# Hybrid SSD and pooling decoder step: the first transfers and splits in smaller pieces, warm-up matmuls between the first real ones

## The chip, the cores and the metric

The kernel runs on one core of a Trainium2 chip. The metric is the device time of one execution in microseconds (us), the median of several runs. The engines are named as in the profile: PE (TensorE: matmuls, with PEld for its weight loads), DVE (VectorE), ACT (ScalarE), POOL (GpSimd) and SP (SyncE, which issues nearly all DMAs here). A granted clock of 1.00 is PE's full speed.

## What is computed

One inference step of a one-layer decoder with two branches: a Mamba-2 style state-space branch (SSD) and a causal pooling branch, joined by sigmoid gates. There are 336 token rows (16 meta, 256 prompt, 64 sample). What matters here is the beginning: the tokens, weighted by `norm_w`, are multiplied by the input projection.

```
h = concat(meta_tokens, x_prompt), x_sample          # 336 rows x 2048
xn = h * rsqrt(mean(h*h) + 1e-6) * norm_w
proj = xn @ w_in                                     # 2048 -> 13344 columns
z_ssd, xbc, dt_raw, z_pool, u, gates = split(proj)
xbc -> causal conv (4 taps), silu -> xs, B, C
dt = softplus(dt_raw + dt_bias); SSD scan over xs, B, C, dt; group norm, w_proj_ssd
pooling means over 2, 4, 8, 16 rows of u; mix, scale, silu(z_pool), w_proj_pool
out = rms_norm(h + (gate_ssd * branch_ssd + gate_pool * branch_pool) @ w_out)
```

## The kernel before

All weights are cut into units of 128 output columns. A unit has 2048 input rows, that is 16 tiles k of 128, and is stored in two halves of 8 tiles (128 x 1024 f32, 512 KB). The order of the units is fixed in `UNITS`; the first are B 0 to 3, C 0 to 3, then xs.

Products are made nearly exact by splitting. A weight half `raw` is rounded by ACT to fp32r (`hi`, line 145), and DVE subtracts to get the rest (`lo`, line 151). The tokens, in 16 tiles of 128 x 336 (`xg`, four tiles in each of four groups; shown as x in the profile), are scaled by `norm_w` and split in the same way into `wh` and `wl`, shown as xh and xl (lines 238 to 249): tile 4q of a group on DVE, the other three on ACT, and all four rests on DVE. Each product of a unit with a tile is three matmuls: hi with xh, hi with xl, lo with xh.

The row scale 1/rms is applied only to the results, so the matmuls can begin before the sum of squares is known. That sum (`sq`, lines 284 to 292) is formed later and read by PE in `ps_sumx` (line 163), in the middle of unit 2.

Units 0 and 1 are run together (lines 251 to 279). For each group q of four tiles PE does 24 matmuls into `acc2`, then four f32 matmuls with the small weight `wdt` for the step sizes, into `psd` (shown as ps_dt). From unit 2 on the loop at the end of the function runs one unit after the other and prepares weights ahead (`prep_hi`, `prep_lo`, `load_to`).

The order on each engine is that of the program (`manual_schedule`), and each engine works through its own list in order, waiting on semaphores where data is missing. SP keeps at most eight of these DMAs under way: from the ninth on, each waits in the compiled program for the DMA eight places before it. The pools `raw`, `hi` and `lo` have four buffers each, so the load of unit 2's first half waits until the first `raw` has been read for the last time.

Before the data is there, PE runs `NWARM` matmuls of a matrix of ones (lines 224 and 225, shown as ps_warm). A copy of that result into `pbs` (line 259) on DVE keeps them in use; `pbs` is overwritten later (line 865).

Of the kernel before, what the change touches and what calls it, by code (L numbers as in the profile page):

```python
# [67 lines left out]
def hybrid_step(tc, ctx, io):  # L68
    nc = tc.nc
    V, S, PE, GP, SY = nc.vector, nc.scalar, nc.tensor, nc.gpsimd, nc.sync  # L70

# [69 lines left out]

    def prep_hi(i, h):
        r = raws[i, h]
        hi = wp.tile([128, HW], F32R, tag="hi", name=f"hi{i}_{h}")
        S.activation(hi, r, AF.Copy)  # L145
        whl[i, h] = hi

    def prep_lo(i, h):
        r, hi = raws.pop((i, h)), whl[i, h]
# [1 line left out]
        V.tensor_tensor(out=lo, in0=r, in1=hi.bitcast(F32), op=ALU.subtract)  # L151
# [60 lines left out]
    load_to(3)
    SY.dma_start(out=xg[2], in_=io["xT"][:, 8:12, :])
    load_to(4)
    SY.dma_start(out=xg[3], in_=io["xT"][:, 12:16, :])
# [5 lines left out]
    load_to(7)  # L221
    V.memset(ones, 1.0)
    warm = ps.tile([128, 512], F32, tag="st", name="ps_warm")
    for j in range(NWARM):
        PE.matmul(warm[:, 0:128], lhsT=ones, rhs=ones, start=(j == 0), stop=(j == NWARM - 1))
# [12 lines left out]
    def split_hi(q):
        for c in range(4):
            k = 4 * q + c  # L240
            if c:
                S.activation(wh[q][:, c, :], xg[q][:, c, :], AF.Copy, scale=pc("norm_w", k))
            else:
                V.tensor_scalar(out=wh[q][:, c, :], in0=xg[q][:, c, :], scalar1=pc("norm_w", k), scalar2=None, op0=ALU.mult)

    def split_lo(q):
        for c in range(4):
            V.scalar_tensor_tensor(out=wl[q][:, c, :], in0=xg[q][:, c, :], scalar=pc("norm_w", 4 * q + c),
                                   in1=wh[q][:, c, :].bitcast(F32), op0=ALU.mult, op1=ALU.subtract)

    for q in range(4):
        h = q // 2
        if q == 0:
# [5 lines left out]
            V.tensor_copy(out=pbs, in_=warm[:, 0:16])
# [2 lines left out]
        else:
            split_hi(q)
            if q < 3:
                prep_hi(q - 1, 1)
            split_lo(q)
            if q < 3:
                prep_lo(q - 1, 1)
        for part in range(3):
            for u in range(2):  # L270
                w = whl[u, h]
                for c in range(4):
                    k = 4 * q + c
                    cc = slice(128 * (k % 8), 128 * (k % 8) + 128)
                    PE.matmul(acc2[u][:, :T], lhsT=w[part // 2][:, cc], rhs=(wl if part == 1 else wh)[q][:, c, :],  # L275
                              start=(k == 0 and part == 0), stop=(k == 15 and part == 2))
        for c in range(4):
            PE.matmul(psd[32 * c:32 * c + 32, :T], lhsT=wdt[:, 4 * q + c, :], rhs=xg[q][:, c, :], start=(q == 0),
                      stop=(q == 3), skip_group_check=True, tile_position=(0, 32 * c))
# [794 lines left out]
```

## Time and profile before

| what | value |
| --- | --- |
| median of 3 runs | 1217.36 us (1216.51 to 1217.37) |
| profiled execution: time / span | 1220.42 / 1218.6 us |
| mean granted PE clock | 0.991 |
| PE busy | 1197.0 us (98%) |
| DVE busy | 739.4 us (61%) |
| ACT busy | 540.1 us (44%) |
| first warm-up matmul, first real matmul | 1.06 us, 7.20 us |
| DMA | 202.49 MB, mean 166 GB/s |

The page gives the busy time of each engine, and then the chain of work that ended last, followed back from the last instruction. The timeline lists instructions in order of time with the idle time ahead of them and what ended it; an f32 matmul is two records in it, an fp32r matmul one. Busy times of PE include the modelled tail of a pipelined matmul, about 0.3 us, so the start of the next one tells more than a duration.

### The profile page before, as it was taken

The page shows a single profiled execution, that of the slowest core. Times are in us where ns is not written, and L with a number is a line of the kernel's source. Part 1 is how long each engine was busy: PE and PEld are TensorE (multiplying, and loading weights), DVE is VectorE, ACT ScalarE, POOL GpSimd, SP SyncE. Part 2 cuts the span into 40 slices and gives each one's busy share as a digit, 9 for nine tenths or more (in the row PEclk, how much of TensorE's full clock was granted, in tenths as well). Part 3 has the DMA queues.
Part 4 walks back from the last instruction along what each step waited for, and adds up shares of the span by engine and source line. Part 5 has one row for each costly group of instructions (what it writes and reads, how often), then busy time and mean ns, then how long its engine had stood idle before and what let it go on. Part 6 is the DMA issues. An engine that isn't in the chain of part 4 may idle for free.

```text
span 1218.6 us, 19976 instructions
## 1 busy us (share of the span) xinstructions
PE 1197.0 (98%) x8124; PEld 1169.4 (96%) x8124; DVE 739.4 (61%) x1141; ACT 540.1 (44%) x735; POOL 105.2 (9%) x107
## 2 busy tenths in 40 slices
PE   8999999999999999999999999999999999999995
PEld 7999999888899999999999999999999999999995
DVE  7786998987885643443457475665354355554443
ACT  6455746474754533333233443434443333334441
POOL 0001151625161000000000000000000000000000
PEclk9999999998999999999999999999999999999997
DMA  7555556574655444444456455454444444455432
GB/s 279 181 159 172 182 169 240 161 247 150 247 174 179 140 155 151 145 154 152 144 172 167 153 155 162 149 166 156 149 146 156 150 146 155 151 189 197 150 111 86
DMA packets 83075, 202.49 MB, mean 166 GB/s; under 512 B 26615, under 2 KB 31639, under 8 KB 82967
## 3 DMA queue, kind: packets, MB, share of 16 engines
q1 hardware_dynamic: 82823, 200.19, 49.2%
q8 instruction: 63, 1.03, 0.3%
q0 software_dynamic: 160, 1.03, 0.2%
q14 instruction: 29, 0.24, 0.1%
HBM read 186.34 MB, written 15.32 MB: 165 GB/s over the span
## 4 chain that ended last, share of the span: by engine, by line
PE 85%; DVE 6%; DMA 4%; issue 2%; ACT 1%; POOL 1%; SPq 0%; DVEq 0%; POOLq 0%
PE acc L231 27%; PE acc L230 27%; PE acc L232 27%; DMA bc<-acT 3%; DVE lo L151 2%; PE acc L275 1%; DVE cacc L337 1%; DMA raw<-wall 1%; DVE M L547 1%; DVE hin L646 1%; DVE hn L969 0%; DMA ossms<-hin 0%; POOL hin L638 0%; PE ps_y L593 0%; PE ps_hn L644 0%
## 5 line engine op out<-in xcount | busy, mean ns | idle before, releaser
L145 ACT ACTIVATE hi<-raw 128x1024 fp32r<-128x1024 f32 x312 | 330.2, 1059 | 542.6 <-PE acc L231 387.5
L151 DVE TENSOR_TENSOR lo<-raw,hi 128x1024 fp32r<-128x1024 f32 x312 | 387.0, 1241 | 258.9 <-ACT hi L145 258.9
L230 PE MATMUL acc<-xh,hi 128*128 128x320 f32 (+4 forms) x1632 | 511.2, 313 | 0.0
L231 PE MATMUL acc<-xl,hi 128*128 128x320 f32 (+4 forms) x1632 | 508.5, 312 | 0.0
L232 PE MATMUL acc<-xh,lo 128*128 128x320 f32 (+4 forms) x1632 | 507.2, 311 | 0.0
L230 PEld LDWEIGHTS acc<-xh,hi 128*128 128x128 f32 x1632 | 307.4, 188 | 2.5 <-issue 0.8
L231 PEld LDWEIGHTS acc<-xl,hi 128*128 128x128 f32 x1632 | 307.3, 188 | 1.1
L232 PEld LDWEIGHTS acc<-xh,lo 128*128 128x128 f32 x1632 | 307.6, 188 | 0.0
L230 PE MATMUL acc<-mh,hi 128*128 128x320 f32 x256 | 79.2, 309 | 0.0
L231 PE MATMUL acc<-ml,hi 128*128 128x320 f32 x256 | 79.1, 309 | 0.0
L232 PE MATMUL acc<-mh,lo 128*128 128x320 f32 x256 | 79.1, 309 | 0.0
L231 PE MATMUL acc<-pl,hi 128*128 128x320 f32 x256 | 79.0, 308 | 0.0
L231 PE MATMUL acc<-yl,hi 128*128 128x320 f32 x256 | 78.9, 308 | 0.0
L232 PE MATMUL acc<-yh,lo 128*128 128x320 f32 x256 | 78.9, 308 | 0.0
L232 PE MATMUL acc<-ph,lo 128*128 128x320 f32 x256 | 78.9, 308 | 0.0
L230 PE MATMUL acc<-yh,hi 128*128 128x320 f32 x256 | 78.9, 308 | 0.0
L230 PE MATMUL acc<-ph,hi 128*128 128x320 f32 x256 | 78.9, 308 | 0.0
L638 POOL TENSOR_TENSOR hin<-hin,E 128x512 f32<-128x512 f32 x32 | 49.7, 1581 | 42.5 <-ACT E L556 42.5
L337 DVE SCALAR_TENSOR_TENSOR cacc<-rawf,par,cacc 128x360 f32<-128x360 f32 (+1 forms) x72 | 48.2, 669 | 1.8
L231 PEld LDWEIGHTS acc<-ml,hi 128*128 128x128 f32 x256 | 48.1, 188 | 0.0
L230 PEld LDWEIGHTS acc<-mh,hi 128*128 128x128 f32 x256 | 48.1, 188 | 0.0
L231 PEld LDWEIGHTS acc<-pl,hi 128*128 128x128 f32 x256 | 48.1, 188 | 0.0
(222 smaller groups left out, 1215.3 us busy)
## 6 DMA issues: line engine op xcount, KB each, us to landing
raw<-wall SPq DMA_DIRECT2D x312, 512.0 KB, 3.3
hin<-ssmT SPq DMA_DIRECT2D x16, 512.0 KB, 6.4
ossms<-hin SPq DMA_DIRECT2D x16, 512.0 KB, 5.6
bc<-acT SPq DMA_DIRECT2D x8, 672.0 KB, 7.2
hn<-xT SPq DMA_DIRECT2D x4, 640.0 KB, 7.7
x<-xT SPq DMA_DIRECT2D x3, 672.0 KB, 9.3
opool<-u SPq DMA_DIRECT2D x16, 100.0 KB, 3.0
oconv<-rawf SPq DMA_DIRECT2D x24, 45.5 KB, 4.1
```

The lines of the kernel that those rows point to most:

```text
L145: S.activation(hi, r, AF.Copy)
L151: V.tensor_tensor(out=lo, in0=r, in1=hi.bitcast(F32), op=ALU.subtract)
L230: PE.matmul(acc[:, :n], lhsT=hi[:, c], rhs=bh, start=first, stop=False)
L231: PE.matmul(acc[:, :n], lhsT=hi[:, c], rhs=bl, start=False, stop=False)
L232: PE.matmul(acc[:, :n], lhsT=lo[:, c], rhs=bh, start=False, stop=last)
L275: PE.matmul(acc2[u][:, :T], lhsT=w[part // 2][:, cc], rhs=(wl if part == 1 else wh)[q][:, c, :], start=(k == 0 and part == 0), stop=(k == ...
L337: V.scalar_tensor_tensor(out=a[:, a0:], in0=r[:, a0 + k:k + ACCW], scalar=pc("conv_w", 4 * c + k), in1=a[:, a0:], op0=ALU.mult, op1=ALU.add)
L547: V.tensor_scalar(out=m[:n, e, o:o + hi - lo], in0=b[:n, hh % 4, lo:hi], scalar1=act_[:n, i, h0 + hh:h0 + hh + 1], scalar2=0.0, op0=ALU.su ...
L638: GP.tensor_tensor(out=hv, in0=hv, in1=E, op=ALU.mult)
L646: later(1, lambda: V.tensor_tensor(out=h, in0=h, in1=p, op=ALU.add))
```

## The change

It touches only what stands ahead of unit 2:

- `par` is loaded in two pieces: the 16 columns of `norm_w` first, the other 264 after all x tiles.
- The first halves of units 0 and 1 and then their second halves are loaded and split in pieces of 512 columns (four k tiles), alternating between the units. The x tiles come singly (0 and 1) or in pairs.
- Splits are issued per quarter and per x tile, in the order in which the matmuls use them.
- `NWARM` goes from 16 to 11. Twelve more warm-up matmuls stand each behind one real matmul of x tiles 0 and 1, six more behind those of tiles 2 and 3. The copy into `pbs` stays behind the last of them.
- In group 0 the order is by pairs of tiles, then unit, then part; in the later groups by part, pair and unit. The step-size matmuls of group 0 move behind group 1.

```diff
-NACC, NTR, NWARM = 3, 3, 16
+NACC, NTR, NWARM = 3, 3, 11
...
-    SY.dma_start(out=par, in_=io["par"])
-    load_to(1)
-    SY.dma_start(out=xg[0][:, 0:2, :], in_=io["xT"][:, 0:2, :])
-    SY.dma_start(out=xg[0][:, 2:4, :], in_=io["xT"][:, 2:4, :])
-    load_to(2)
-    SY.dma_start(out=xg[1], in_=io["xT"][:, 4:8, :])
+    def load_x(k, n):
+        SY.dma_start(out=xg[k // 4][:, k % 4:k % 4 + n, :], in_=io["xT"][:, k:k + n, :])
+
+    def load_part(i, h, a):
+        if not a:
+            raws[i, h] = wp.tile([128, HW], F32, tag="raw", name=f"raw{i}_{h}")
+        SY.dma_start(out=raws[i, h][:, 512 * a:512 * a + 512], in_=io["wall"][i, h, :, 512 * a:512 * a + 512])
+
+    SY.dma_start(out=par[:, 0:16], in_=io["par"][:, 0:16])
+    load_part(0, 0, 0)
+    load_x(0, 1)
+    load_x(1, 1)
+    load_part(1, 0, 0)
+    load_x(2, 2)
+    load_part(0, 0, 1)
+    load_part(1, 0, 1)
+    load_x(4, 2)
+    load_x(6, 2)
     SY.dma_start(out=wdt, in_=io["wdt"])
...
+    for j in range(2):
+        load_part(0, 1, j)
+        load_part(1, 1, j)
+        load_x(8 + 4 * j, 2)
+        load_x(10 + 4 * j, 2)
+    SY.dma_start(out=par[:, 16:NPAR], in_=io["par"][:, 16:NPAR])
+    nload[0] = 4
...
-    for j in range(NWARM):
-        PE.matmul(warm[:, 0:128], lhsT=ones, rhs=ones, start=(j == 0), stop=(j == NWARM - 1))
+    def turn_over(n):
+        for j in range(n):
+            PE.matmul(warm[:, 0:128], lhsT=ones, rhs=ones, start=True, stop=True)
+    turn_over(NWARM)
...
     for q in range(4):
-        h = q // 2
         if q == 0:
-            prep_hi(0, 0)
-            split_hi(0)
-            prep_hi(1, 0)
-            split_lo(0)
-            prep_lo(0, 0)
+            w_hi(0, 0)
+            x_hi(0)
+            x_lo(0)
+            x_hi(1)
+            w_lo(0, 0)
+            x_lo(1)
+            w_hi(1, 0)
+            w_lo(1, 0)
+            x_hi(2)
+            x_lo(2)
+            x_hi(3)
+            x_lo(3)
+            for k, u in ((0, 0), (0, 1), (2, 0), (2, 1)):
+                for part in range(3):
+                    for d in range(2):
+                        mm(u, k + d, part)
+                        if k == 0:
+                            turn_over(1)
+            turn_over(6)
             V.tensor_copy(out=pbs, in_=warm[:, 0:16])
-            prep_lo(1, 0)
+        else:
+            for u in range(2):
+                w_hi(u, q)
+                w_lo(u, q)
+            for k in range(4 * q, 4 * q + 4):
+                x_hi(k)
+                x_lo(k)
+            for part in range(3):
+                for k in range(4 * q, 4 * q + 4, 2):
+                    for u in range(2):
+                        mm(u, k, part)
+                        mm(u, k + 1, part)
+        if q == 1:
             V.tensor_tensor(out=wdt, in0=wdt, in1=par[:, o:o + 16].unsqueeze(2).to_broadcast([128, KT, NH]), op=ALU.mult)
...
+        for e in ((), (0, 1), (2,), (3,))[q]:
+            for c in range(4):
+                PE.matmul(psd[32 * c:32 * c + 32, :T], lhsT=wdt[:, 4 * e + c, :], rhs=xg[e][:, c, :], start=(e == 0),
+                          stop=(e == 3), skip_group_check=True, tile_position=(0, 32 * c))
```

`x_hi`, `x_lo`, `w_hi` and `w_lo` are the old splits for one x tile or one quarter, and `mm` is one matmul.

What stands where, on the two engines that matter. Names read as tile, unit or group, half: raw0_0 is unit 0, first half; xh1 is group 1. On PE at its beginning, before:

```order
L225 MATMUL ps_warm_135<-ones_79 128x128 x16
L275 MATMUL acc0_153<-xh0_101,hi0_0_155 128x336 x4
L275 MATMUL acc1_154<-xh0_101,hi1_0_161 128x336 x4
L275 MATMUL acc0_153<-xl0_105,hi0_0_155 128x336 x4
L275 MATMUL acc1_154<-xl0_105,hi1_0_161 128x336 x4
L275 MATMUL acc0_153<-xh0_101,lo0_0_167 128x336 x4
L275 MATMUL acc1_154<-xh0_101,lo1_0_170 128x336 x4
```

and in the changed kernel, the first five rows of that place:

```order
L242 MATMUL ps_warm_144<-ones_79 128x128 x11
L282 MATMUL acc0_157<-xh0_101,hi0_0_159 128x336
L242 MATMUL ps_warm_144<-ones_79 128x128
L282 MATMUL acc0_157<-xh0_101,hi0_0_159 128x336
L242 MATMUL ps_warm_144<-ones_79 128x128
```

The alternation goes on through twelve real matmuls. Where it ends, on PE of the changed kernel:

```order
L242 MATMUL ps_warm_144<-ones_79 128x128
L282 MATMUL acc0_157<-xh0_101,hi0_0_159 128x336 x2
L282 MATMUL acc0_157<-xl0_105,hi0_0_159 128x336 x2
L282 MATMUL acc0_157<-xh0_101,lo0_0_160 128x336 x2
L282 MATMUL acc1_158<-xh0_101,hi1_0_163 128x336 x2
L282 MATMUL acc1_158<-xl0_105,hi1_0_163 128x336 x2
L282 MATMUL acc1_158<-xh0_101,lo1_0_164 128x336 x2
L242 MATMUL ps_warm_144<-ones_79 128x128 x6
L282 MATMUL acc0_157<-xh1_102,hi0_0_159 128x336 x2
```

Six warm-ups now stand between group 0 and group 1, where the step-size matmuls of group 0 stood. On DVE, around the copy into `pbs`, before:

```order
L244 TENSOR_SCALAR xh0_101<-x0_93,par_77 128x336
L248 SCALAR_TENSOR_TENSOR xl0_105<-x0_93,par_77,xh0_101 128x336 x4
L151 TENSOR_TENSOR lo0_0_167<-raw0_0_110,hi0_0_155 128x1024
L259 COPY pbs_87<-ps_warm_135 128x16
L151 TENSOR_TENSOR lo1_0_170<-raw1_0_114,hi1_0_161 128x1024
L261 TENSOR_TENSOR wdt_92<-wdt_92,par_77 128x512
L244 TENSOR_SCALAR xh1_102<-x1_94,par_77 128x336
```

and in the changed kernel:

```order
L264 SCALAR_TENSOR_TENSOR xl0_105<-x0_93,par_77,xh0_101 128x336 x2
L306 COPY pbs_87<-ps_warm_144 128x16
L278 TENSOR_TENSOR lo0_0_160<-raw0_0_110,hi0_0_159 128x512
L278 TENSOR_TENSOR lo1_0_164<-raw1_0_114,hi1_0_163 128x512
L261 TENSOR_SCALAR xh1_102<-x1_94,par_77 128x336
L264 SCALAR_TENSOR_TENSOR xl1_106<-x1_94,par_77,xh1_102 128x336 x4
L320 TENSOR_TENSOR wdt_92<-wdt_92,par_77 128x512
```

The copy stands between the last rest of group 0 and the first subtraction for group 1, and it reads a tile that the six warm-ups above write.

More of the change, by code (lines that the diff above doesn't have):

```diff
@@ L204, in hybrid_step @@
     wl = [slot(f"xl{q}", [128, 4, T], F32R) for q in range(4)]
-    SY.dma_start(out=par, in_=io["par"])
-    load_to(1)
-    SY.dma_start(out=xg[0][:, 0:2, :], in_=io["xT"][:, 0:2, :])
-    SY.dma_start(out=xg[0][:, 2:4, :], in_=io["xT"][:, 2:4, :])
-    load_to(2)
-    SY.dma_start(out=xg[1], in_=io["xT"][:, 4:8, :])
-    SY.dma_start(out=wdt, in_=io["wdt"])
[L212 to L215, printed above, removed]
+    def load_x(k, n):
[14 more added lines that the diff above has]
+    load_x(6, 2)
+    SY.dma_start(out=wdt, in_=io["wdt"])
+    for j in range(2):
[5 more added lines that the diff above has]
+    nload[0] = 4
     SY.dma_start(out=ident, in_=io["ident"])
@@ L236, in hybrid_step, with x_hi @@
     o = _PC["norm_w"][0]
[L238 to L249, printed above, removed]
+    def x_hi(k):
+        o = wh[k // 4][:, k % 4, :]
+        if k % 4:
+            S.activation(o, xg[k // 4][:, k % 4, :], AF.Copy, scale=pc("norm_w", k))
+        else:
+            V.tensor_scalar(out=o, in0=xg[k // 4][:, k % 4, :], scalar1=pc("norm_w", k), scalar2=None, op0=ALU.mult)
@@ new lines, in x_lo, with w_hi @@
+    def x_lo(k):
+        V.scalar_tensor_tensor(out=wl[k // 4][:, k % 4, :], in0=xg[k // 4][:, k % 4, :], scalar=pc("norm_w", k),
+                               in1=wh[k // 4][:, k % 4, :].bitcast(F32), op0=ALU.mult, op1=ALU.subtract)
+    for u in range(2):
+        for h in range(2):
+            whl[u, h] = tuple(wp.tile([128, HW], F32R, tag=t, name=f"{t}{u}_{h}") for t in ("hi", "lo"))
+    def w_hi(u, q):
+        c = slice(512 * (q % 2), 512 * (q % 2) + 512)
+        S.activation(whl[u, q // 2][0][:, c], raws[u, q // 2][:, c], AF.Copy)
@@ L251, in hybrid_step, with w_lo, mm @@
+    def w_lo(u, q):
+        c = slice(512 * (q % 2), 512 * (q % 2) + 512)
+        hi, lo = whl[u, q // 2]
+        V.tensor_tensor(out=lo[:, c], in0=raws[u, q // 2][:, c], in1=hi[:, c].bitcast(F32), op=ALU.subtract)
+    def mm(u, k, part):
+        w = whl[u, k // 8][part // 2][:, 128 * (k % 8):128 * (k % 8) + 128]
+        PE.matmul(acc2[u][:, :T], lhsT=w, rhs=(wl if part == 1 else wh)[k // 4][:, k % 4, :],
+                  start=(k == 0 and part == 0), stop=(k == 15 and part == 2))
     for q in range(4):
-        h = q // 2
@@ L253, in hybrid_step @@
         if q == 0:
-            prep_hi(0, 0)
-            split_hi(0)
-            prep_hi(1, 0)
-            split_lo(0)
-            prep_lo(0, 0)
-            V.tensor_copy(out=pbs, in_=warm[:, 0:16])
-            prep_lo(1, 0)
-            V.tensor_tensor(out=wdt, in0=wdt, in1=par[:, o:o + 16].unsqueeze(2).to_broadcast([128, KT, NH]), op=ALU.mult)
[L262 to L279, printed above, removed]
+            w_hi(0, 0)
@@ new lines, in hybrid_step @@
+            turn_over(6)
+            V.tensor_copy(out=pbs, in_=warm[:, 0:16])
+        else:
+            for u in range(2):
[6 more added lines that the diff above has]
+                for k in range(4 * q, 4 * q + 4, 2):
+                    for u in range(2):
+                        mm(u, k, part)
+                        mm(u, k + 1, part)
+        if q == 1:
+            V.tensor_tensor(out=wdt, in0=wdt, in1=par[:, o:o + 16].unsqueeze(2).to_broadcast([128, KT, NH]), op=ALU.mult)
@@ L280, in hybrid_step @@
+        for e in ((), (0, 1), (2,), (3,))[q]:
+            for c in range(4):
+                PE.matmul(psd[32 * c:32 * c + 32, :T], lhsT=wdt[:, 4 * e + c, :], rhs=xg[e][:, c, :], start=(e == 0),
+                          stop=(e == 3), skip_group_check=True, tile_position=(0, 32 * c))
+    for u in range(2):
+        for h in range(2):
+            raws.pop((u, h))
     for u in range(2):
```

## Prediction

> **What bounds the kernel now.** I read the page's busy shares and its chain first, then the first 35 us on each engine in order of time, then busy time and clock by windows.
>
> ```profile
> PE 85%; DVE 6%; DMA 4%; issue 2%; ACT 1%; POOL 1%; SPq 0%; DVEq 0%; POOLq 0%
> ```
>
> PE (TensorE) carries the chain, so a microsecond gained before the first steady unit counts only if PE keeps it to the end. The timeline of PE at the start (start, duration, line, tiles, records, in brackets the idle time before and its releaser):
>
> ```profile
> 5.76 0.72 PE L225 MATMUL ps_warm<-ones 128*128 128x128 f32 x5
> 7.20 0.55 PE L275 MATMUL acc<-xh,hi 128*128 128x336 f32 x2 [0.71 <-DVE xh L244]
> 8.56 0.89 PE L275 MATMUL acc<-xh,hi 128*128 128x336 f32 x2 [0.82 <-ACT xh L242]
> 10.33 0.89 PE L275 MATMUL acc<-xh,hi 128*128 128x336 f32 x4 [0.88 <-ACT hi L145]
> 11.05 2.26 PE L275 MATMUL acc<-xl,hi 128*128 128x336 f32 x8
> ...
> 15.85 1.50 PE L275 MATMUL acc<-xh,hi 128*128 128x336 f32 x8
> ...
> 19.75 0.77 PE L278 MATMUL ps_dt<-x,wdt 128*32 128x336 f32 x8
> 20.45 1.50 PE L275 MATMUL acc<-xh,hi 128*128 128x336 f32 x8
> ...
> 25.06 1.50 PE L275 MATMUL acc<-xh,hi 128*128 128x336 f32 x8
> ...
> 29.66 0.42 PE L230 MATMUL acc<-xh,hi 128*128 128x336 f32 x1
> ```
>
> PE waits three times before 10.33 and never after it; unit 2 begins at 29.66. That instant is the quantity I forecast. From 15.85 a group of four x tiles costs 3.90 for its 24 matmuls (15.85 to 19.75) and 0.70 for its step-size matmuls (19.75 to 20.45), 4.60 in all; 25.06 to 29.66 is the same.
>
> ```profile
> 4.00:4.40 0.40, 0.40 (x3) 0.40 (x3) 0.00 (x0) 0.00 (x0) 0.00 (x0) 1.00 1.05 306
> 4.40:4.80 0.40, 0.40 (x6) 0.40 (x5) 0.00 (x0) 0.20 (x1) 0.00 (x0) 1.00 1.06 370
> ...
> 4.46:7.86 3.40, 2.57 (x20) 2.13 (x19) 1.17 (x3) 1.63 (x2) 0.00 (x0) 1.00 0.95 327
> 7.86:11.26 3.40, 1.77 (x8) 1.30 (x9) 2.99 (x6) 2.45 (x4) 0.00 (x0) 1.00 1.00 408
> 11.26:14.66 3.40, 3.40 (x14) 3.40 (x13) 3.36 (x7) 2.38 (x5) 0.00 (x0) 0.50 1.03 422
> ```
>
> Columns: window, length, busy of PE, weight loads, DVE, ACT, POOL, then granted clock, DMA share, GB/s. Warm-up records double their pace near 4.4 (3, then 6 in 0.40 us). After a stretch with PE 76% busy (2.57 of 3.40) the clock stays 1.00; after one at 52% (1.77) it is 0.50 for 3.40 us, which costs about 1.7 us of matmul time. So before has two losses to win: the waits up to 10.33 and this half clock.
>
> **The change, part by part.** *Transfers.* Landings before, read where ACT had waited for them:
>
> ```profile
> 4.60 1.06 ACT L145 ACTIVATE hi<-raw 128x1024 fp32r<-128x1024 f32 x1 [2.58 <-DMA raw<-wall]
> 6.64 0.57 ACT L242 ACTIVATE xh<-x,par 128x336 fp32r<-128x336 f32 x1 [0.98 <-DMA x<-xT]
> 7.94 1.04 ACT L242 ACTIVATE xh<-x,par 128x336 fp32r<-128x336 f32 x2 [0.72 <-DMA x<-xT]
> 9.22 1.06 ACT L145 ACTIVATE hi<-raw 128x1024 fp32r<-128x1024 f32 x1 [0.24 <-DMA raw<-wall]
> 10.91 1.04 ACT L242 ACTIVATE xh<-x,par 128x336 fp32r<-128x336 f32 x2 [0.63 <-DMA x<-xT]
> ```
>
> These five had 652, 988, 1324, 1836 and 2508 KB ordered up to their ends (par 140, raw 512, x 336 twice, raw 512, x 672). In the new order x tile 0 ends at 432 KB and tile 1 at 600, both below 652, so in by 4.6; unit 1's quarter ends at 856 (about 5.8), x 2 and 3 at 1192 (7.4), the second quarters at 1448 and 1704 (8.3, 8.9), x 4 to 7 at 2376 (10.6). SP issues nine more DMAs by then, and keeps eight in flight, about 2 MB, so it stays ahead of the data. Its load of unit 2's first half waits for the DVE subtraction that frees the buffer (near 14.6, 10.7 before), but SP reaches it only then, when the eighth DMA ahead of it (x 10 and 11, near 14.5 by the same pace) has landed. Behind it stand two mask loads and later weights, which nobody needs before 23. The quarter and single splits on ACT cost more fixed time; ACT waits for data throughout (the brackets above) and hides it.
>
> *First real matmul.* NWARM falls by 5 matmuls, 10 records. The five records from 5.76 last 0.72, of which the last one's modelled length is about 0.3, so they start 0.105 apart. The stream would have given way at 6.29; ten records earlier is **5.24**. By then xh 0 is split (4.6 plus 0.39), so PE need not wait.
>
> *Interleaved warm-ups.* No row before shows one f32 matmul between two fp32r ones. The nearest is a group of three:
>
> ```profile
> 39.56 0.32 PE L232 MATMUL acc<-xh,lo 128*128 128x336 f32 x1
> 39.71 0.83 PE L182 MATMUL ps_rsx<-dgx,ones 128*128 128x128 f32 x6
> 40.30 0.40 PE L230 MATMUL acc<-xh,hi 128*128 128x336 f32 x1
> 40.54 0.32 PE L231 MATMUL acc<-xl,hi 128*128 128x336 f32 x1
> ```
>
> A real matmul takes 0.155; the six records take 0.59 (0.196 a matmul), and the next real one 0.24 in place of 0.155, so 0.085 for the switch. One warm-up then costs 0.28 and a pair 0.435. Bounds: 0.365 (0.155 and two records of 0.105) if the switch is free, 0.52 if it is paid both ways. I take 0.435, the row's own: 12 pairs are 5.22, to 10.46. The data is ahead at that pace: lo of unit 1 is needed near 9.1 and done near 7.5; xl 3 is needed near 11, done near 9.1. The 12 real matmuls of x 2 and 3 are 1.86 (12.32), six more warm-ups 12 records of 0.105, 1.26 (**13.58**).
>
> *The copy on DVE.* DVE works in order, and its copy of `ps_warm` into `pbs` now stands behind the six last warm-ups, with the whole second group queued behind it. Before:
>
> ```profile
> 10.64 0.17 DVE L259 COPY pbs<-ps_warm 128x16 f32<-128x16 f32 x1
> 10.73 1.22 DVE L151 TENSOR_TENSOR lo<-raw,hi 128x1024 fp32r<-128x1024 f32 x1
> ...
> 12.46 0.39 DVE L244 TENSOR_SCALAR xh<-x,par 128x336 fp32r<-128x336 f32 x1
> 12.88 2.01 DVE L248 SCALAR_TENSOR_TENSOR xl<-x,par,xh 128x336 fp32r<-128x336 f32 x4
> ```
>
> There the warm-ups had ended four microseconds earlier and the copy took 0.09. Now DVE, idle from about 9.1, gets past it only when PE's last warm-up has landed. How soon after, and what a 512-wide subtraction takes, come from:
>
> ```profile
> 33.48 0.72 PE L163 MATMUL ps_sumx<-ones,sq 128*128 128x1 f32 x6
> ...
> 29.90 0.51 DVE L292 TENSOR_TENSOR sq<-sq 128x336 f32<-128x336 f32 x1
> 30.32 1.22 DVE L151 TENSOR_TENSOR lo<-raw,hi 128x1024 fp32r<-128x1024 f32 x1
> 31.46 0.17 DVE L865 TENSOR_TENSOR pbs<-par 128x16 f32<-128x16 f32 x1
> ...
> 34.24 0.16 DVE L168 TENSOR_SCALAR srx<-ps_sumx 128x3 f32<-128x3 f32 x1 [0.34 <-PE ps_sumx L163]
> ```
>
> DVE follows PE's modelled end (34.20) by 0.04; with the last record's 0.3 against its 0.105 slot the copy starts at 13.82. A subtraction of 336 columns holds DVE 0.42, one of 1024 1.14, so 512 about 0.60 by the line between them (bounds 0.42 and 1.14). Copy 0.09, two subtractions 1.20, xh 4 0.39: 15.50. PE's first matmul of the second group needs xh 4 and starts 0.15 later (7.20 against 6.66 plus 0.39): **15.65**. PE has stood still for two microseconds, and xl 4 to 7 follow at 0.49 each (12.88, four in 2.01), just ahead of PE.
>
> *The rest.* The second group 3.90, two step-size blocks (the first is moved here) 1.40, then 4.60 and 4.60: 15.65 + 3.90 + 1.40 + 9.20 = **30.15**, against 29.66: 0.5 us later. Both losses of before are gone, and 18 added warm-ups (5 taken from the front) and the copy's wait take their place.
>
> *What is late next.* DVE ends xl 15 near 25.3, then lo of unit 2 and the sum of squares, done near 32.4; PE wants that sum for ps_sumx at 30.15 + 3.82 = 33.97. The 1.6 us that are left cover it; lo of unit 2's second half, near 33.6, has 1.2. The later stages shift as a whole.
>
> The profiled execution took 1220.42 with a span of 1218.6; the median of the runs is 1217.36. The shift is the same in each, so 1217.36 + 0.5 = **1217.9**. Pairs at 0.365 make it 0.8 less, at 0.52 1.0 more; the subtraction's bounds give 0.4 less to 1.1 more. I use 1217.0 to 1219.0 as the forecast's own range.
>
> **The rivals.**
>
> *The clock falls in the new gap (slower).* Place: PE idle from about 13.8 to 15.65. The clock changed near 4.4, 11.26, 14.66, and, by the rows below, at 280.9, which is 78 steps of 3.413 later. On that grid (11.26, 14.67, 18.09) the gap is split into about 0.9 and 0.95, so each window is 71 to 74% busy, near the 76% that kept full clock. If the gap falls into one window, that is 46% busy, under the 52% that lost it. A second place shows what it costs:
>
> ```profile
> 281.08 1.44 PE L163 MATMUL ps_sumg<-ones,ss 128*128 128x1 f32 x6 [2.90 <-POOL ss L685]
> ...
> 280.00:281.00 1.00, 0.00 (x0) 0.95 0.97 291
> ...
> 287.00:288.00 1.00, 1.00 (x6) 0.63 0.00 0
> ```
>
> A wait of 2.90 us brought half clock from 280.9 to 287.7. One window at half costs 1.2 to 1.7: 30.15 becomes 31.35 to 31.85, 1219.1 to 1219.6. It decides once t(copy) moves by 0.4 us either way. The Trainium skill, "TensorE: Matmul & The Clock Gate", section "What's actually happening", has half rate return after at least one idle window of about 3.4 us; by that a gap of two microseconds costs nothing and the sum stays. The trace speaks against it: it fell after a window 52% busy, which is why I give this a good chance.
>
> *The small transfers are slow (slower).* Mechanism: unit 2's first weights come late, and with them ACT's squares, DVE's sum and ps_sumx. About 6070 KB stand up to their end, as before.
>
> ```profile
> 19.87 1.06 ACT L145 ACTIVATE hi<-raw 128x1024 fp32r<-128x1024 f32 x1 [0.88 <-PE acc L275]
> ```
>
> From the start of that tile's split to the end of the sum (29.90 plus 0.51 above) it was 10.5 us, so the split must begin by 23.4: below some 300 GB/s from 1.9 us on, PE waits. At 250 it begins near 27.4, 4 us late: 1221.8. Against it stand 1280-byte rows, the nearest to the new 1344 and 2048:
>
> ```profile
> 1096.00:1097.00 1.00, 1.00 1.06 383
> ...
> hn<-xT SPq DMA_DIRECT2D x4, 640.0 KB, 7.7
> ```
>
> 383 GB/s with small rows. It was 640 KB a transfer, so the smaller size itself stays untested. The Trainium skill, "DMA: Bandwidth & Descriptors", section "Rules for kernel authors", wants at least 1 MiB per DMA, and its section "Bandwidth" has 138 GB/s at 64 KB against 341 at 1 MB; by that, 256 KB would run between, an estimate that lands in this rival. The trace's row speaks against so large a loss.
>
> *The copy does not hold DVE.* If the wait is met earlier than I read it, PE runs on at 13.58: 13.58 + 3.90 + 1.40 + 9.20 = 28.08, 1.6 us earlier, 1215.8. Against it: the copy reads the tile that all warm-ups write, and the last six stand ahead of it.
>
> *The later gap of 2.90 us meets the windows otherwise.* A shift of a microsecond or more could spare one half-clock window there, 1.7 us: 1216.2.
>
> **How the numbers follow.** Forecast 0.50; clock 0.28; slow transfers 0.07; copy without effect 0.08; later gap 0.07. What can be told from no change is 0.2%, 2.4 us: below 1214.9 or above 1219.8. Faster needs the third rival with cheap pairs or with the fourth: 0.05. Slower: the transfers 0.07, a third of the clock rival 0.09, the forecast's upper bounds 0.03: 0.19. Same 0.76. The range 1216.1 to 1219.9 leaves out the transfers, the copy rival and the ends of the clock rival, some 0.2.
>
> **What would show it.** The first real matmul near 5.2; the copy on DVE waiting for PE over 4 us, to 13.8; PE idle about 1.9 us before the matmul of x 4 at 15.65; PEclk 1.00 from 11 to 22; unit 2 at 30.15; ps_sumx without a wait. A copy that starts at 9 or a unit 2 before 28.5 proves me wrong on the gain, a wait at ps_sumx on the transfers.

## The result and the profile after

| | before | changed |
| --- | --- | --- |
| median of 6 runs | 1217.11 us (1216.26 to 1217.37) | 1223.80 us (1221.31 to 1226.55) |
| profiled execution: time / span | 1220.42 / 1218.6 us | 1226.55 / 1224.8 us |
| mean granted PE clock | 0.991 | 0.989 |
| unit 2 starts on PE | 29.66 us | 32.35 us |

The ratio is 1.0052, 95% interval 1.0040 to 1.0064: slower by half a per cent, well outside the range that was given. In the profiles the spans differ by 6.2 us. Unit 2 begins 2.69 us later, and 3.5 us more are lost behind it. Both profiled executions took some 3 us more than the medians, so what they show is an example and not the average. Here and below a rare execution that ran far longer (one of 1350.99 us at a granted clock of 0.813 was the profiled one of shift_bc7) is left out of the ratios, and that profile is not used.

The timeline of PE at the start of the changed kernel (start, duration, line, tiles, records, idle time before and its releaser):

```profile
5.03 0.40 PE L282 MATMUL acc<-xh,hi 128*128 128x336 f32 x1
...
7.07 0.42 PE L282 MATMUL acc<-xh,hi 128*128 128x336 f32 x1 [1.42 <-ACT xh L259]
...
11.23 0.55 PE L282 MATMUL acc<-xh,hi 128*128 128x336 f32 x2
...
13.15 1.50 PE L242 MATMUL ps_warm<-ones 128*128 128x128 f32 x12
16.51 1.47 PE L282 MATMUL acc<-xh,hi 128*128 128x336 f32 x8 [1.86 <-DVE xh L261]
17.82 2.40 PE L282 MATMUL acc<-xl,hi 128*128 128x336 f32 x8
20.02 1.96 PE L282 MATMUL acc<-xh,lo 128*128 128x336 f32 x8
21.91 1.34 PE L323 MATMUL ps_dt<-x,wdt 128*32 128x336 f32 x16
...
32.35 0.42 PE L248 MATMUL acc<-xh,hi 128*128 128x336 f32 x1
```

The first real matmul starts at 5.03 and the second waits 1.42 us for the split of x tile 1. From 7.07 to 11.23 the pairs run 0.378 us apart. Behind the six trailing warm-ups PE is idle for 1.86 us, and then the eight matmuls at 17.82 need 2.20 us where the eight at 16.51 needed 1.31.

DVE in the changed kernel, around the copy:

```profile
14.69 0.17 DVE L306 COPY pbs<-ps_warm 128x16 f32<-128x16 f32 x1 [4.23 <-PE ps_warm L242]
14.78 1.28 DVE L278 TENSOR_TENSOR lo<-raw,hi 128x512 fp32r<-128x512 f32 x2
15.98 0.39 DVE L261 TENSOR_SCALAR xh<-x,par 128x336 fp32r<-128x336 f32 x1
```

The copy waits for PE, and two subtractions (0.60 us each) and xh 4 follow it, as forecast: 1.82 us from the copy to PE's restart, where 1.83 were given.

ACT, and then busy time by windows (window, length, busy of PE, weight loads, DVE, ACT, POOL, granted clock, DMA share, GB/s):

```profile
3.97 0.63 ACT L273 ACTIVATE hi<-raw 128x512 fp32r<-128x512 f32 x1 [1.95 <-DMA raw<-wall]
6.44 0.57 ACT L259 ACTIVATE xh<-x,par 128x336 fp32r<-128x336 f32 x1 [1.84 <-DMA x<-xT]
```

```profile
4.00:5.00 1.00, 1.00 (x10) 1.00 (x10) 0.48 (x2) 0.60 (x1) 0.00 (x0) 1.00 1.06 134
5.00:6.00 1.00, 0.65 (x6) 0.45 (x4) 1.00 (x2) 0.00 (x0) 0.00 (x0) 1.00 0.52 173
...
0.00:6.40 6.40, 4.59 (x25) 4.39 (x25) 1.73 (x4) 1.91 (x2) 0.34 (x6) 1.00 0.58 152
```

ACT, free since 4.60, gets x tile 1 at 6.44. That tile ends 600 KB into the order of the loads, but 152 GB/s over 6.40 us are some 950 KB: bytes that stand behind it had already moved. Counting bytes in order of issue does not date a landing here.

The windows of the clock, 3.41 us long, cut where it changed:

```profile
4.21:7.62 3.41, 1.99 (x16) 1.80 (x16) 2.13 (x4) 0.97 (x2) 0.00 (x0) 1.00 0.92 234
...
14.45:17.86 3.41, 1.55 (x11) 1.39 (x11) 3.14 (x8) 2.74 (x6) 0.00 (x0) 1.00 1.06 388
17.86:21.28 3.42, 3.42 (x14) 3.42 (x13) 3.38 (x8) 1.62 (x3) 0.00 (x0) 0.50 1.05 388
280.70:284.11 3.41, 0.47 (x4) 0.20 (x2) 3.38 (x4) 2.53 (x4) 3.41 (x3) 1.00 0.22 47
284.11:287.52 3.41, 1.04 (x5) 1.04 (x6) 1.60 (x3) 1.47 (x2) 3.41 (x4) 0.50 0.74 250
287.52:290.94 3.42, 3.42 (x18) 2.75 (x19) 1.10 (x3) 0.56 (x2) 3.42 (x4) 0.50 0.04 16
290.94:294.35 3.41, 3.41 (x15) 3.41 (x14) 3.27 (x7) 0.00 (x0) 3.41 (x5) 0.50 0.27 36
```

The gap behind the copy fell almost whole into the window from 14.45 to 17.86: 45% busy, and the next window ran at half clock. The wait for x 1 left its window 58% busy and cost no clock. At 284 there were three half windows, two in before. What stands ahead of them, on PE, and on SP in the changed kernel and in the kernel before:

```profile
286.48 1.44 PE L163 MATMUL ps_sumg<-ones,ss 128*128 128x1 f32 x6 [5.30 <-POOL ss L733]
```

```profile
254.82 5.85 SPq L490 DMA_DIRECT2D hin<-ssmT  x2
...
261.27 0.38 SPq L485 DMA_DIRECT2D bc<-acT  x1
```

```profile
251.69 5.06 SPq L442 DMA_DIRECT2D hin<-ssmT  x2
...
257.62 0.36 SPq L437 DMA_DIRECT2D bc<-acT  x1
```

SP holds its loads of `hin` (SSD states) until the store `ossms` of the same buffer has landed (it waited 4.3 us for that before, 5.0 changed), and `bc` (the decay rows for DVE) stands behind them. DVE, ACT and POOL work from `bc` toward `ss`, which PE wants at ps_sumg, the sums for the group norm: 5.30 us late, 2.90 before. The first DVE instructions that read this `bc`, before and then in the changed kernel:

```profile
263.89 1.36 DVE L547 TENSOR_SCALAR M<-bc,acum 128x256 f32<-128x256 f32 x6 [3.06 <-DMA bc<-acT]
```

```profile
269.29 1.36 DVE L595 TENSOR_SCALAR M<-bc,acum 128x256 f32<-128x256 f32 x6 [4.30 <-DMA bc<-acT]
```

Against the beginning of unit 2 they start 2.71 us later in the changed kernel: `bc` is issued 0.96 us later, and it takes 8.02 us from there to DVE instead of 6.27. Why the transfer itself took longer is not known. From ps_cb, the first product of the SSD, (118.08 before, 120.76 changed: +2.68, no change since unit 2), to ps_sumg the changed kernel takes 2.72 us more, 2.40 of it this wait, and from there to the last group's ps_cb 0.53 more.

### The profile page after: what moved, and what is told of

The parts are those of the page before. It is cut to its first block, busy times and chain, and to the rows that moved or that the text cites. A ratio compares the mean times of both kernels' runs of the same rounds, so it can differ in the third digit from the quotient of the medians.

```text
span 1224.8 us, 20055 instructions
## 1 busy us (share of the span) xinstructions
PE 1199.7 (98%) x8150; PEld 1172.8 (96%) x8150; DVE 740.0 (60%) x1145; ACT 541.6 (44%) x739; POOL 105.9 (9%) x107
## 4 chain that ended last, share of the span: by engine, by line
PE 88%; DVE 5%; DMA 3%; issue 1%; POOL 1%; ACT 0%; SPq 0%; DVEq 0%; POOLq 0%
PE acc L248 28%; PE acc L249 28%; PE acc L250 28%; DMA bc<-acT 2%; PE acc L282 1%; DVE lo L151 1%; DMA raw<-wall 1%; PE ps_y L641 1%; DVE cacc L385 1%; DVE M L595 1%; DVE hn L1017 0%; DVE hin L694 0%; PE ps_hn L692 0%; POOL hin L686 0%; PE ps_yo L653 0%
## 5 line engine op out<-in xcount | busy, mean ns | idle before, releaser
L145 ACT ACTIVATE hi<-raw 128x1024 fp32r<-128x1024 f32 x308 | 326.0, 1059 | 543.8 <-PE acc L249 395.6
L151 DVE TENSOR_TENSOR lo<-raw,hi 128x1024 fp32r<-128x1024 f32 x308 | 382.8, 1243 | 257.7 <-ACT hi L145 257.7
L249 PEld LDWEIGHTS acc<-yl,hi 128*128 128x128 f32 x256 | 48.1, 188 | 0.0
L248 PEld LDWEIGHTS acc<-ph,hi 128*128 128x128 f32 x256 | 48.1, 188 | 0.0
L248 PEld LDWEIGHTS acc<-yh,hi 128*128 128x128 f32 x256 | 48.1, 188 | 0.0
```

The source lines that it names most:

```text
L248: PE.matmul(acc[:, :n], lhsT=hi[:, c], rhs=bh, start=first, stop=False)
L249: PE.matmul(acc[:, :n], lhsT=hi[:, c], rhs=bl, start=False, stop=False)
```

## The experiments

Each was run beside the kernel before, and the ratio is to that. Unit 2, the wait of ps_sumg for POOL near 280 us and the span are from the one profiled execution, which need not be typical: those of copy_late, pair_bc7 and shift_bc7_b took 2.8 to 5.6 us more than the median of their runs.

| run | unit 2 | wait at ps_sumg | span | median | ratio (95%) |
| --- | --- | --- | --- | --- | --- |
| before_again | 28.04 | 3.56 | 1216.2 | 1217.98 | one run |
| shift12 | 30.99 | 4.67 | 1219.5 | 1221.42 | 1.0034 (1.0022 to 1.0046) |
| copy_late | 31.00 | 5.14 | 1221.5 | 1220.50 | 1.0022 (1.0012 to 1.0032) |
| copy_late_nowarm | 27.12 | 4.05 | 1218.2 | 1220.35 | 1.0018 (1.0007 to 1.0028) |
| after_again | 32.25 | 4.01 | 1222.4 | 1223.45 | 1.0037 (1.0024 to 1.0050) |
| big_loads | 32.72 | 3.97 | 1221.8 | 1223.49 | 1.0033 (1.0021 to 1.0045) |
| after_bc | 30.11 | none | 1220.4 | 1221.65 | 1.0025 (1.0013 to 1.0037) |
| before_bc | 27.12 | 0.27 | 1212.4 | 1214.18 | 0.9967 (0.9948 to 0.9986) |
| before_bc7 | 27.98 | 0.28 | 1210.7 | 1212.46 | 0.9958 (0.9943 to 0.9973) |
| after_bc7 | 31.26 | 0.28 | 1215.9 | 1217.93 | 1.0005 (0.9988 to 1.0022) |
| lead_warm | 28.71 | 3.68 | 1216.4 | 1220.04 | 1.0019 (1.0007 to 1.0030) |
| pair_bc7 | 25.44 | 0.28 | 1218.4 | 1214.63 | 0.9976 (0.9963 to 0.9990) |
| before_bc7_b | 27.49 | 0.25 | 1209.7 | 1211.45 | 0.9945 (0.9926 to 0.9964) |
| shift_bc7 | – | – | – | 1216.90 | 0.9986 (0.9972 to 1.0001) |
| shift_bc7_b | 30.60 | 0.26 | 1219.1 | 1215.54 | 0.9984 (0.9974 to 0.9994) |
| after_bc7_b | 32.42 | none | 1217.6 | 1218.69 | 1.0004 (0.9987 to 1.0022) |
| big_bc7 | 32.91 | 0.27 | 1215.7 | 1218.27 | 1.0006 (0.9990 to 1.0023) |

**The start of before, again, and a plain delay.** before_again is the kernel before. shift12 adds twelve warm-ups to it between groups 0 and 1:

```diff
+        if q == 1:
+            for j in range(12):
+                PE.matmul(warm[:, 0:128], lhsT=ones, rhs=ones, start=True, stop=True)
```

> The kernel before, unchanged, for a second profile: unit 2 begins on PE at 29.4 to 29.9, ps_sumg of the first group waits for POOL 2.9 us (2.5 to 3.5 if that wait is fixed by the order of the work; anything from 1 to 6 if it is chance).

> The kernel before with 12 more f32 matmuls of ones on PE between groups 0 and 1, and nothing else: unit 2 begins about 2.6 us later (24 records of 0.105 and 0.085). Theory 'a late start costs only itself': total 2.6 us over before (1.5 to 3.5), the wait at ps_sumg stays at 2.9. Theory 'a late start is paid twice, because a store and a broadcast in the SSD stage meet other DMAs': 5 to 7 us over before, wait at ps_sumg 5. Theory 'the later loss belongs to the new load order': 2.6 us.

Before_again starts unit 2 at 28.04 and has no half clock in its first stage. The same holds for three later profiles with before's start unaltered (before_bc 27.12, before_bc7 27.98, before_bc7_b 27.49); only the one that the prediction was made from has 29.66. The half clock that the change was to remove belonged to that execution: PE's three waits up to 10.33 add up to 2.41 us there, most of it in one window, and the same waits to 1.15 to 1.63 in the four others. shift12 puts unit 2 at 30.99, 3.0 us behind before_again, and its ratio is worth 4 us: more than the delay alone, less than the 5 to 7 of the theory that it is paid twice.

**The copy out of the way.** In copy_late the copy into `pbs` stands behind group 3:

```diff
             turn_over(6)
-            V.tensor_copy(out=pbs, in_=warm[:, 0:16])
...
+    V.tensor_copy(out=pbs, in_=warm[:, 0:16])
```

In copy_late_nowarm the 18 warm-ups between and behind the first real matmuls go as well.

> The changed kernel with the copy of ps_warm into pbs moved behind group 3, so that DVE waits for nothing there; all warm-ups stay. Theory 'the copy's wait and the half clock behind it made the late start': no idle PE before group 1, clock 1.00 from 5 to 22, unit 2 at 28.9 (11.23 + 1.9 + 1.3 + 3.9 + 1.3 + 9.2), 3.4 us earlier than in the changed kernel; total 3 to 7 us below the changed kernel, near before. Rival 'the late x tile and the loads bind': unit 2 not before 31, total above 1221.

> As copy_late, and without the 18 warm-ups between and behind the first real matmuls (the 11 at the front stay). Theory 'warm-ups displace real work': unit 2 earlier than in copy_late by 1 to 3 us, and ps_sumx becomes the next wait (sum of squares done near 31). Rival 'warm-ups hold the clock': the clock falls to 0.50 for one window between 8 and 15 and unit 2 comes no earlier than in copy_late.

PE of copy_late, and its clock windows:

```profile
8.01 0.65 PE L282 MATMUL acc<-xh,hi 128*128 128x336 f32 x1 [2.37 <-ACT xh L259]
...
15.48 1.50 PE L242 MATMUL ps_warm<-ones 128*128 128x128 f32 x12
16.73 1.47 PE L282 MATMUL acc<-xh,hi 128*128 128x336 f32 x8
```

```profile
4.17:7.58 3.41, 1.47 (x13) 1.28 (x11) 1.57 (x3) 0.64 (x2) 0.00 (x0) 1.00 0.87 226
7.58:10.99 3.41, 2.98 (x13) 2.99 (x13) 2.85 (x5) 3.08 (x6) 0.00 (x0) 0.50 1.04 401
```

The gap behind the warm-ups is gone, so the copy made it. But x tile 1 came later still in this execution: 2.37 us of waiting left the window 43% busy, and the half clock that had stood at 18 us stands at 7.6. Unit 2 begins at 31.00. Without the 18 warm-ups it begins at 27.12, again after a half clock (from 7.87), so they cost some 3.5 us of PE here (x 1 came 0.4 us earlier) and saved no half clock. But ps_sumx then waits 0.54 us for DVE's sum, and the time stays 2 us above before. Two places, the wait for x 1 and the copy, can each cost the clock.

**Both places covered.** lead_warm is copy_late with 16 leading warm-ups, which last until x 1 is there.

```diff
-NACC, NTR, NWARM = 3, 3, 11
+NACC, NTR, NWARM = 3, 3, 16
```

> The changed kernel with the copy of ps_warm behind group 3 and with 16 leading warm-ups instead of 11, so that they last until x tile 1 has landed; the 18 inner ones stay. Theory that two gaps alone made the half clock (the wait for x 1 and the wait behind the copy): first real matmul at 6.2 to 6.6, no wait over 1 us up to 20 us, no half clock there, pairs end near 11.0, group 1 at 14.2 without a gap, unit 2 at 28.3 to 29.0, about that of before, and the time within 1.5 us of before. Rival, that the order of matmuls or splits itself costs: unit 2 after 30.

PE of lead_warm:

```profile
6.74 0.40 PE L282 MATMUL acc<-xh,hi 128*128 128x336 f32 x1
...
14.44 1.47 PE L282 MATMUL acc<-xh,hi 128*128 128x336 f32 x8
...
28.71 0.42 PE L248 MATMUL acc<-xh,hi 128*128 128x336 f32 x1
```

No wait, no half clock, and unit 2 inside its interval of 28.3 to 29.0. So the two waits made the half clock, and the rival that the order of splits and matmuls costs (unit 2 after 30) is out. What is left is a start 0.7 to 1.6 us behind the four profiles of before's start without half clock. The median is still 2 us above before, where 1.5 was the bound, so part of the loss stands behind unit 2.

**The loads.** after_again is the changed kernel once more. big_loads has its order of work with the loads of before (halves of 512 KB, x in 2, 2, 4, 4 and 4 tiles).

> The changed kernel itself once more, beside the next three. If the loss behind the first stages is chance, the time from unit 2 to the end differs from the profiled run of after by more than a microsecond, and the ratio to before may come out at 1.002 to 1.004 (start alone: unit 2 near 31 to 32.4 against 28 to 29.7). If it is systematic, x tile 1 lands at 6.4 to 7.4 again, half clock falls into the first 22 us again, the wait of ps_sumg for POOL is 4 us or more again (before: 2.90 and 3.56), and the ratio is 1.004 to 1.006.

> The changed order of splits and matmuls with the loads of before (whole halves of 512 KB, x in 2, 2, 4, 4, 4 tiles, par in one piece). Theory that small transfers move slowly at first: the window 2 to 3 us goes back from 156 to near 296 GB/s, 0 to 6.4 us from 152 to near 212. x 0 and 1 then land as one pair at 6.6 to 7.0, as in before, so the wait of PE for x moves ahead of the first real matmul, the pairs end at about 11.5 instead of 11.23, and the start comes out no earlier: unit 2 within 0.7 us of the same kernel with small loads at the same clock (30.8 with full clock, 32.3 with one half-clock window). Rival, that one-tile loads themselves cost PE its 1.4 to 2.4 us: x is there by 5 us, PE has no wait over 0.3 us up to the copy, and unit 2 begins at 29.0 to 29.6.

ACT of big_loads, its windows, and PE's first real matmul:

```profile
6.04 0.57 ACT L252 ACTIVATE xh<-x,par 128x336 fp32r<-128x336 f32 x1 [0.47 <-DMA x<-xT]
```

```profile
4.00:5.00 1.00, 1.00 (x8) 1.00 (x8) 0.00 (x0) 0.06 (x1) 0.00 (x0) 1.00 0.97 363
5.00:6.00 1.00, 0.49 (x5) 0.30 (x3) 0.00 (x0) 0.57 (x1) 0.00 (x0) 1.00 1.08 406
```

```profile
6.60 0.39 PE L275 MATMUL acc<-xh,hi 128*128 128x336 f32 x1 [1.11 <-DVE xh L254]
```

after_again repeats the changed kernel: x 1 at 6.35, half clock from 17.88, unit 2 at 32.25, 4.01 us at ps_sumg, so the loss is not chance. In big_loads the dip at 4 to 6 us (134 and 173 GB/s) is gone (363 and 406), so the small transfers do move slowly there. Size alone is not the reason: from 8 to 9 us the changed kernel's small transfers move 402 GB/s. And the changed kernel wants fewer bytes first (600 KB up to x 1, against 988), so the two effects cancel: x 0 and 1 land at 6.04 as a pair against 6.44 for x 1 alone, the wait moves ahead of the first real matmul, unit 2 begins at 32.72 and the time is that of after_again. By the Trainium skill, "DMA: Bandwidth & Descriptors", section "Rules for kernel authors", transfers should be of 1 MiB or more. The rates from 4 to 6 us point the same way, though no transfer here is that large; the 402 GB/s from 8 us on and the time do not.

**The wait at ps_sumg.** after_bc and before_bc issue hin 2 and 3 two steps later, behind `bc`. before_bc7 and after_bc7 put only hin 3 behind it.

```diff
-        plan += [(4 + q // 2 + q // 2, lambda q=q: hin_load(q)) for q in range(4)]
+        plan += [(4 + 4 * (q // 2), lambda q=q: hin_load(q)) for q in range(4)]
```

and for the second pair

```diff
-                        later(1, lambda: bc_load(1))
+                        later(1, lambda: (bc_load(1), hin_load(3)))
...
-        plan += [(4 + q // 2 + q // 2, lambda q=q: hin_load(q)) for q in range(4)]
+        plan += [(4 + q // 2 + q // 2, lambda q=q: hin_load(q)) for q in range(3)]
```

> The changed kernel with the loads hin 2 and 3 of each SSD group issued four steps after hin 0 and 1 instead of two, so that the load of bc no longer stands behind hin's wait for the store of ossms. Theory that this wait makes PE's gap at ps_sumg and the half clock behind it, and with them the part of the loss that grows behind unit 2: bc is issued some 6 us earlier, the wait of ps_sumg falls from 5.30 to under 1 us, no half clock from 280 to 300, and the time is 5 to 9 us below after. Rival, that the wait is set by something else (ACT's squares, POOL): the wait at ps_sumg stays within 1 us of 5.3 and the time within 2 us of after.

> The same edit on the kernel before. Theory: the wait of 2.90 to 3.56 at ps_sumg falls under 1 us, its two half-clock windows go, the time is 3 to 7 us below before; and the difference between after_bc and before_bc is that of unit 2 alone, 2 to 4 us. Rival: within 2 us of before, and the pair differs by 5 us or more as the two kernels themselves do.

> Before with only the load of hin 3 put behind that of bc; hin 2 stays ahead of it. Theory that bc late behind hin's wait for the store makes the gap at ps_sumg: that wait is under 1 us as in before_bc (0.27), PE's waits for hin at ps_yo (0.45 and 0.25 in before_bc) go as well, time 1212 to 1215. Rival, that hin 2 also holds bc back: the wait at ps_sumg is 2 us or more and the time 1216 to 1218. It is also one more sample of before's start, which this edit doesn't touch: unit 2 at 27.1 to 28.1 without half clock, or near 29.7 with it.

> The same on the changed kernel. Theory that behind unit 2 both kernels differ only by how the transfers meet: PE's waits for hin (0.74 and 1.43 in after_bc) and the 2.18 at ps_sumg of the last group shrink, and what is left between this and before_bc7 is the start, 2 to 4.5 us (unit 2 at 30.1 to 32.4 against 27.1 to 29.7). Rival, that the changed loads put the later transfers at a lasting disadvantage: the difference is 6 us or more, as between after_bc and before_bc (7.5).

The wait is gone in all four (0.28 or less), with the half clock behind it, so it was `bc` queued behind hin's wait for the store. The time did not follow everywhere. after_bc is only 1.8 us below after_again, run beside it, and not 5 to 9: PE now waits at ps_yo, the product with `hin` (0.74 and 1.43 us), and 2.18 us at the last ps_sumg, with a half-clock window at each of the two places. On the kernel before that gives 0.9958 with hin 3 alone: this version beats both. On the changed kernel it gives 1.0005. The expectation that only the start would be left between the two did not hold: 5.5 us are left (7.5 between after_bc and before_bc). PE's remaining waits, in before_bc7:

```profile
259.33 1.05 PE L605 MATMUL ps_yo<-hin,Cs 128*32 128x512 f32 x4 [0.34 <-DMA hin<-ssmT]
275.52 0.83 PE L163 MATMUL ps_sumg<-ones,ss 128*128 128x1 f32 x6 [0.28 <-POOL ss L685]
...
317.02 0.83 PE L163 MATMUL ps_sumg<-ones,ss 128*128 128x1 f32 x6 [0.34 <-POOL ss L685]
```

and in after_bc7:

```profile
263.88 1.05 PE L653 MATMUL ps_yo<-hin,Cs 128*32 128x512 f32 x4 [1.62 <-DMA hin<-ssmT]
280.08 0.83 PE L163 MATMUL ps_sumg<-ones,ss 128*128 128x1 f32 x6 [0.28 <-POOL ss L733]
...
322.24 0.83 PE L163 MATMUL ps_sumg<-ones,ss 128*128 128x1 f32 x6 [1.02 <-POOL ss L733]
```

3.28 at unit 2, 1.28 at ps_yo and 0.68 at the last ps_sumg make 5.24; the spans differ by 5.2.

after_bc has a use of its own. Its start is that of the changed kernel, and the windows fell otherwise there. PE, then the windows:

```profile
6.39 0.42 PE L282 MATMUL acc<-xh,hi 128*128 128x336 f32 x1 [0.15 <-ACT xh L259]
...
15.83 1.47 PE L282 MATMUL acc<-xh,hi 128*128 128x336 f32 x8 [1.86 <-DVE xh L261]
...
30.11 0.42 PE L248 MATMUL acc<-xh,hi 128*128 128x336 f32 x1
```

```profile
12.27:15.68 3.41, 1.70 (x15) 1.51 (x13) 1.67 (x4) 2.53 (x6) 0.00 (x0) 1.00 1.05 403
15.68:19.09 3.41, 3.26 (x21) 3.29 (x22) 3.38 (x8) 2.98 (x7) 0.00 (x0) 1.00 1.06 388
```

These windows are cut back from the edges of its next half clock, at 264.86 and 268.27. x 1 landed early (0.15 us of waiting), the same gap of 1.86 us cost no clock although most of it lies in one window (PE 50% busy), and unit 2 begins at 30.11, where the prediction had 30.15.

**What follows a late start.** These runs were to find the other 2 us: the pair again, the kernel before_bc7 delayed by 13 warm-ups as in shift12, and the changed order with the loads of before.

> The kernel before with hin 3 behind bc, again, as the base of the next three: 1211.5 to 1214.5, unit 2 at 27 to 28.1.

> The same with 13 f32 warm-ups between groups 0 and 1, a delay of 3.2 us by the 2.95 of twelve. If a late start costs only itself: 3 to 3.8 us above before_bc7_b. If a late start also makes later transfers miss: 5 us or more, with PE's wait for hin at ps_yo over 1 us near 260.

> The changed kernel with hin 3 behind bc, again. If the 2 us behind the start were chance: 3 to 4.2 us above before_bc7_b. If they last: 5 us or more.

> The changed order of splits and matmuls with the loads of before, and hin 3 behind bc. If the small first loads make the later transfers late: 1.5 us or more below after_bc7_b, though unit 2 comes no earlier. If the order of work makes the loss: within 1 us of after_bc7_b.

> The same kernel as shift_bc7, for its profile. If a late start makes later transfers miss: unit 2 at 30.3 to 31.2, and behind it PE's waits for hin (0.34 and 0.49 near 259 us in before_bc7) and for POOL at the last ps_sumg (0.34) add up to 1.5 us or more above those, with or without a half clock. If it costs only itself: these waits as in before_bc7, and the median nearer 1215.

big_bc7 is within 0.5 us of after_bc7_b: the loads are not to blame. The plain delay gives no clear answer. shift_bc7 came out at 1216.90, 5.4 us above before_bc7_b, but its second run (shift_bc7_b) at 0.9984, against 0.9945 and 0.9958 without the delay, or 3.2 to 4.8 us; the profile shows a start 2.6 to 3.1 us later. So the delay costs 0.1 to 2.8 us more than itself. The profiled execution, 5.4 us above the median of its runs, has these waits:

```profile
262.65 1.05 PE L608 MATMUL ps_yo<-hin,Cs 128*32 128x512 f32 x4 [0.74 <-DMA hin<-ssmT]
...
322.53 1.44 PE L163 MATMUL ps_sumg<-ones,ss 128*128 128x1 f32 x6 [2.58 <-POOL ss L688]
```

The last of them brought half clock from 322.1 to 328.9. In the three profiles with the early start and `bc` ahead the wait at the last ps_sumg was 0.34 to 0.35; in the late ones it was 0.68 (after_bc7_b), 1.02, 2.18 (after_bc), 2.21 (big_bc7) and 2.58. Taken by the two pairs, 5.5 and 7.2 us between the medians stand against 3.3 and 4.9 us at unit 2, and between after_again and before_again 6.2 us of span against 4.2: the changed kernel loses about 2 us more behind its start. That the late start alone makes this, whatever caused it, is what these waits suggest; it is not shown. Why the transfers near 260 and 300 us don't move along with PE was not settled.

**An attempt at both.** pair_bc7 has x 0 and 1 in one transfer ahead of the weights, 15 leading warm-ups, none between or behind the first real matmuls, the late copy and hin 3 behind `bc`.

> A combination that may beat both: x 0 and 1 in one transfer ahead of the first quarter of the weights, 15 leading warm-ups, none between real matmuls, the copy behind group 3, and hin 3 behind bc. First real matmul at 6.0 to 6.8, no half clock in the first 25 us, unit 2 at 25 to 27; ps_sumx then waits 0.5 to 2 us for DVE's sum (ready near 31.1 to 31.6), so that little of it is kept: time 1212 to 1215, within 1.5 us of before_bc7. Against it: x 4 to 7 land after 11 us, so group 1 may wait and lose the clock; then unit 2 comes at 27 to 28 and the time is 1 to 2 us more.

```profile
32.24 1.44 PE L163 MATMUL ps_sumx<-ones,sq 128*128 128x1 f32 x6 [2.82 <-DVE sq L336]
```

Unit 2 begins at 25.44, the earliest of all, and the gain is lost seven microseconds later: the sum of squares is not ready, PE waits 2.82 us and the clock is at half from 32.0 to 38.9. This execution took 5.6 us more than the median of its runs, so a wait of that size is not the rule; by the medians the kernel is slower than before_bc7 by 2 us. The sum also comes later here than in the kernel before: DVE has it at 31.6 to 33.2 us in copy_late, copy_late_nowarm, lead_warm, pair_bc7 and the changed kernel, at 29.4 to 30.4 in the five profiles with before's start. ps_sumx comes 3.8 us behind the beginning of unit 2, so with these splits a start ahead of about 28 is not kept.

## Why the prediction was wrong

The forecast of unit 2 was 30.15, the profile has 32.35. At the start two steps failed, the landing of x tile 1 and the clock in the gap; behind it two more, that the later stages shift as a whole and that one profile's shift is that of the median. Step by step:

- *First real matmul* at 5.24: right in kind, 5.03.
- *Landing of x tile 1* (by 4.6, from the bytes ordered ahead of it): failed. It landed at 6.44, and between 5.76 and 7.38 in the other profiles with the same loads. The second real matmul started at 7.07 in place of 5.68: +1.40.
- *Pairs at 0.435*: mis-sized, 0.378, near the low bound. Eleven pairs: -0.63. That the twelve reals and the warm-ups behind them differ by 0.06 shows that the other durations held.
- *The copy holds DVE, and DVE holds PE*: right, 3.36 us from the end of the reals to the restart against 3.33. The rival that the copy would not wait is out.
- *The gap would be split between windows and keep full clock*: failed, and the clock rival came true at its place and price. The place of the gap within the windows was taken from before's grid; it moved by the step above, and the grid itself starts elsewhere in each execution. Group 1 to unit 2 took 15.84 instead of 14.50, of which 1.50 are half clock. Of seven profiles with this gap (the changed kernel and big_loads, with and without the edit to `bc`) five lost the clock, two did not. The chance of 0.28 was too low.
- *Unit 2's sum has 1.6 us to spare*: right; ps_sumx did not wait (the sum was there at 33.21, PE wanted it at 36.17), and the rival of slow small transfers failed at the place where it was put. Slow they were, at 4 to 6 us.
- *The later stages shift as a whole*: failed. Up to the first ps_cb they did (88.4 us from unit 2, in both). Then the load of `bc` was issued 0.96 us later against unit 2 (261.27 less 32.35, 257.62 less 29.66) and took 1.75 us longer to DVE, PE waited 2.40 us more at ps_sumg, and a half-clock window more followed. The rival on that gap had only the sign that gains.
- *The shift is the same for the median*: failed in a way that the profile could not show by itself. The profile of before carried a half clock at the start that four others do not have. Against these (27.7 in the mean) the changed kernel's five starts (32.35, 32.25, 30.11, 31.26 and 32.42, mean 31.7) are 4.0 us late, not 2.7. With the about 2 us that the changed kernel loses behind its start this comes near the measured difference of the medians, 5.2 (after_again) to 6.7 us.

The Trainium skill, "TensorE: Matmul & The Clock Gate", section "What's actually happening", says that its window is free-running and does not begin with the kernel. The profiles agree: the first half clock of five of them starts at 7.58, 7.87, 11.26, 17.86 and 18.33, which are 0.75, 1.04, 1.02, 0.80 and 1.27 past a multiple of 3.413; in after_bc it is 2.03. Its rule that the clock falls after a whole idle window does not hold here: windows 45%, 43% and, in before, 52% busy were enough, though one 50% busy (after_bc) kept full clock.

## What to carry to other kernels

A warm-up matmul whose result a second engine must read in order puts that engine's whole queue behind PE: have it read late, or not at all. Do not date a first landing by counting bytes; take the rows of a transfer of the same place, and keep PE fed until the latest of them. Before a gain is booked from one profile, look whether a loss in it (a half clock above all) is there in a second one, and look at what each later wait behind a store or a load does when the start moves by a few microseconds.

## What was not expected of the hardware

- Cut at the changes of the clock and in steps of 3.413 us from them, the windows of eighteen profiles (all but shift_bc7's) give 22 falls of the clock up to 1190 us, all after PE had been busy for 1.77 of 3.41 us or less (52%). Three windows below that kept it: 1.56 in lead_warm (near 277), 1.70 in after_bc and 1.75 in big_bc7 (near 320). In the last 25 us of the kernels the clock fell after 2.07 (before_bc7) and 2.24 (after_again) as well, where 1.99 at the start of the changed kernel had kept it. A window half idle can be enough, and the busy time alone does not decide.
- After a window at half clock that was wholly busy the full clock came back at 21.28, but at 287.52 to 290.94 a busy window was followed by another at half.
- A single 168 KB load issued at 2.1 us landed at 5.76 to 7.38 in executions with the same loads ahead of it. Rates in the two microseconds from 4 to 6 were 122 to 244 GB/s in the eight profiles with these loads, with transfers of 168 to 336 KB, and 363 to 406 in big_loads and big_bc7, with 336 to 672 KB; from 8 to 9 us the eight moved 371 to 411.
